# Heads of weight chunks, the order of two mixers, and the row counts of the score products in a two-layer decoder trunk

## The chip, the cores and the metric

The kernel runs on one core of a Trainium2 chip. The metric is the device time of one execution in microseconds (us); the time given for a kernel is the median of its runs. TensorE (PE in the profile) multiplies, ScalarE (ACT) and VectorE (DVE) do element-wise work, GpSimd (POOL) as well, and SyncE (SP) issues the transfers of the weights from the chip's main memory. SBUF is the working memory with 128 partitions, PSUM the memory of eight banks into which TensorE writes.

## The reference

The input is 256 rows of 1024 float32 numbers. Two layers follow each other, each made of a feed-forward block, a mixer and another feed-forward block, all with RMS norm ahead of them and added to the running sum; a final norm ends it.

```python
h = x
for layer in range(DEPTH):
    h = h + 0.5 * swiglu(rms_norm(h, ffn1_norm[layer]), ...)
    hn = rms_norm(h, mix_norm[layer])
    h = h + (ab_mixer(hn, ...) if layer % 2 == 0 else c_mixer(hn, ...))
    h = h + 0.5 * swiglu(rms_norm(h, ffn2_norm[layer]), ...)
return rms_norm(h, final_norm)

def swiglu(x, w_gate, w_up, w_down):
    return (jax.nn.silu(x @ w_gate) * (x @ w_up)) @ w_down
```

`swiglu` goes from 1024 to 2816 and back. The first mixer has two halves: causal attention with 8 heads of 64, in which three windows are combined (they become one mask here), and a gating in which 4 groups of 128 channels are mixed over positions and multiplied with a GELU. The second mixer is causal attention with 16 heads of 64; with 256 rows its blocks are one block. Both end in an output projection.

## The kernel before, in words

**Precision.** A product of two float32 matrices is made of three fast products: each operand is split in a high part (a rounded copy, made by ACT) and a low part (what is left, made by DVE), and `mm3` (lines 197 to 200) adds high x high, high x low and low x high in PSUM. Lines 198, 199 and 200 are these three, so most of TensorE's time stands on them in equal parts.

**Weights.** `Stream` (lines 39 to 112) brings the weights in chunks of 2048 numbers per partition (1 MB). `add` lists the chunks in the order of use, `load_one` issues a transfer on SP's queue, `split_parts` makes the high and low tiles (`whi`, `wlo`; lines 86 and 87). Three raw buffers and four pairs of split ones go round: `take` hands out the next chunk, `free` gives it back and starts later ones. A chunk of a column-wise product has 8 blocks k of 128 input rows and 256 columns, that is two tiles of 128 columns; one tile takes 8 x 3 = 24 matmuls of 256 columns, a chunk 48.

**Heads.** A chunk lies shifted by SHIFT = 16 numbers within lines of 64. Some chunks have `reset=3` (a head): their first three k, all 256 columns of them, are put behind the others, at a place 52 numbers into a line (lines 77 to 80). In a feed-forward block these are the chunks named by `again` (lines 140 to 144): 1 and 3 in the first block, 2 and 3 in the next two, 2, 3 and 7 in the last. Other heads lie in the mixers (lines 165, 166 and 177).

**Feed-forward block** (`ffn`, line 427). Chunk n is taken at step n; gate and up chunks take turns, 22 in all. In the blocks after the first, the sums of squares for the norm are made by small matmuls after chunk 1 (`sums`, line 264), and after chunk 2 two transposes spread them over the columns (`spread`, line 282). In the first block transposes of gain vectors with 16 rows (line 373) come after chunk 2 as well, and in the last one sixteen transposes after chunk 6 (line 444). The down projection has 528 matmuls of 256 columns, in the last block products of 512 columns (`finish`).

**Mixers.** Two kinds of products come by turns. `token_block` (line 689) makes 128 rows of positions by 512 columns: 48 matmuls of 512 columns in two chunks; `tile_of` (line 806) makes 128 columns by 256 positions: 24 matmuls of 256. Between them stand the attention's steps: `put_q` and `put_k` take a tile of two heads from PSUM, `scores(h)` multiplies, applies the mask, the exponential and its scaling, `turn(h)` transposes the probabilities, and `weighted(p)` multiplies a pair of heads with v. A dictionary by slot, written out by hand, says at which slot each is issued (lines 768 to 781 and 829 to 834); a slot is a tile, a part of a token block or a step of the projection. Each engine takes its instructions in the order written (a scheduler moves few of them).

**Scores.** A head has 64 channels. `put_q` puts the high and the low part of q in the two halves of 128 partitions; `put_k` makes a tile with the high part of k in both halves and one with the low part in both (two copies each by POOL, lines 624 and 625). Two 128-row products (lines 637 and 638) for each half of the positions then hold all four combinations.

**Output projection** (`project`, line 308). Four steps of 24 matmuls, then four of 12, then the rest; each uses one block of the mixers' outputs, and `after(i)` runs the events of a slot behind step i. `Next.pair` adds the result to the running sum and makes the input of the next block. The first feed-forward chunk of a block is taken in the order `LATE` (line 306), so that the last two k come late.

Of the kernel before, what the change touches and what calls it, by code (L numbers as in the profile page):

```python
# [10 lines left out]
F32 = mybir.dt.float32  # L11
# [26 lines left out]

class Stream:
# [30 lines left out]
    def split_parts(self):  # L70
# [9 lines left out]
        self.parts[j] = tuple([t[:, at(k) : at(k) + w] for k in range(nk)] for t in (his, los))  # L80
        k0 = 0
        for k1 in cuts:
            a, n = at(k0), int((k1 - k0) * w)
            r = raw[:, int(k0 * w) : int(k0 * w) + n]
            hi, lo = his[:, a : a + n], los[:, a : a + n]
            nc.scalar.activation(hi, r, AF.Copy)  # L86
            nc.vector.tensor_sub(lo, r, hi.bitcast(F32))  # L87
            k0 = k1
            yield
# [26 lines left out]
def trunk(ctx: ExitStack, tc: tile.TileContext, a, out):  # L116
# [473 lines left out]
    def make_attention(mp, mask_cols, nheads, v, mix, engine, rows=False):  # L590
# [6 lines left out]
        def scaled(bk):  # L597
            t = mp.tile([128, S], F32, name="qk", bufs=2)
            nc.vector.tensor_mul(t, bk[:, :S], norm["row"])
            return t  # L600

        def put_q(p, bk):

            qq = mp.tile([128, 2 * S + LINE], F32R, name="q", bufs=pairs)
            t = bk[:, :S] if rows else scaled(bk)
            for j in range(2):
                q = qq[:, SHIFT + j * S : SHIFT + (j + 1) * S]
                r = slice(j * 64, j * 64 + 64)
                o = slice(64 - j * 64, 128 - j * 64)
                nc.scalar.activation(q[r, :], t[r, :], AF.Copy)  # L610
                nc.vector.tensor_sub(q[o, :], t[r, :], q[r, :].bitcast(F32))  # L611
                qs[2 * p + j] = q

        def put_k(p, bk):

            t = scaled(bk)
            for j in range(2):
                kh = mp.tile([128, S], F32R, name=f"kh{j}", bufs=pairs)
                kl = mp.tile([128, S], F32R, name=f"kl{j}", bufs=pairs)
                r = slice(j * 64, j * 64 + 64)  # L620
                o = slice(64 - j * 64, 128 - j * 64)
                nc.scalar.activation(kh[r, :], t[r, :], AF.Copy)
                nc.vector.tensor_sub(kl[r, :], t[r, :], kh[r, :].bitcast(F32))  # L623
                nc.gpsimd.tensor_copy(kh[o, :], kh[r, :].bitcast(F32))
                nc.gpsimd.tensor_copy(kl[o, :], kl[r, :].bitcast(F32))
                ks[2 * p + j] = (kh, kl)

        def scores(h):
            q = qs.pop(h)
            kh, kl = ks.pop(h)  # L630
# [53 lines left out]
    def run_events(ev, s):  # L684
        for f in ev.pop(s, []):
            f()


    def token_block(m, evict, step=lambda: None):

        pb = [bank(), bank()]
        for i in range(2):
# [6 lines left out]
            if i == 0 and m == 0:  # L699
                nxt.sums()  # L700
# [11 lines left out]
    def ab_mixer(phase):  # L712
        with tc.tile_pool(name="mp", bufs=1) as mp:
# [38 lines left out]
            token_block(0, lambda t, p: put_v(v, t, p))  # L752
            nxt.spread()
            token_block(1, keep_g)

# [12 lines left out]
            ev = {}  # L768

            def at(s, f, *args):  # L770
                ev.setdefault(s, []).append(lambda: f(*args))

            at(0, turn_spatial)
            for i, s in enumerate((3, 4, 5, 6)):
                at(s, mixing, i)
            for h, s in enumerate((8, 9, 10, 11, 12, 12, 13, 13)):
                at(s, scores, h)
            for h, s in enumerate((11, 11, 12, 13, 14, 14, 15, 15)):
                at(s, turn, h)
            for p, s in enumerate((12, 14, 15, 16)):  # L780
                at(s, weighted, p)

            slot = 0

            def tiles(put):

                nonlocal slot
                w = st.take()
                for j in range(2):
                    p = bank()  # L790
                    tile_of(p, w, j)
                    put(j, p)
                    run_events(ev, slot)
                    slot += 1
                st.free()
# [5 lines left out]
            for put, c in ((put_u, 0), (put_q, 0), (put_u, 1), (put_k, 0), (put_q, 1), (put_k, 1)):  # L801
# [99 lines left out]
```

## Time and profile before

| what | value |
|---|---|
| median of 3 runs | 978.74 us (978.63 to 981.01) |
| the profiled execution by its own time | 977.56 us |
| its span, from the first to the last instruction | 975.8 us |
| mean granted TensorE clock | 0.997 |
| first mixer, with its projection | 196.3 to 294.1 us |
| second mixer, with its projection | 668.0 to 782.9 us |
| the rest | four feed-forward blocks |

The profile is one execution. In the page's first part stand busy time, its share of the span and the number of instructions of each engine; PEld is the loading of weights (of the operand that is held in the array), which overlaps PE. A matmul lasts 0.28 us in the trace, but the next one begins earlier: what counts is the distance between two starts. A row of the timeline has start, length, engine, line, operation, output and inputs, sizes and, in brackets, idle time ahead of it and what ended it. In a row of the windows stand the stretch, its length, busy time and number by engine (PE, PEld, DVE, ACT, POOL), the granted clock, the share of the DMA engines and GB/s. A row of the waits says who waited for whom: total, times and longest. In a group's row stand line, engine, operation, output and inputs, sizes, count, then busy time, the mean of one in ns, and idle time ahead of it.

### The profile page before, as it was taken

Reading aid. Unit: us, or ns where it says so; the run is one execution under the profiler, and the core shown is the slowest. Engines: PE = TensorE matmul, PEld = TensorE weight load, DVE = VectorE, ACT = ScalarE, POOL = GpSimd, SP = SyncE. Lnnn points to the kernel's source line nnn. Section 1 sums busy time; section 2 is a strip of 40 time slices with the busy share of each in tenths; the row PEclk is TensorE's granted clock in tenths of the full one; section 3 lists DMA queues with packets and bytes.
Section 4 is the critical chain, followed back from the end, with each engine's and each line's share of the span. In section 5 each row is a group of like instructions: output and inputs, shape, how many; then the busy total and the mean of one; then the engine's idle time right before and its main releaser. Section 6 shows DMA issues by size and latency. Waiting matters only on the chain.

```text
span 975.8 us, 18069 instructions
## 1 busy us (share of the span) xinstructions
PE 960.6 (98%) x7679; PEld 935.7 (96%) x7679; DVE 614.5 (63%) x867; ACT 504.4 (52%) x784; POOL 68.4 (7%) x98
## 2 busy tenths in 40 slices
PE   9999999999899999999999999999999999999997
PEld 8999999989899999999999999999999999999886
DVE  6856546568877665655665566466888776566443
ACT  7644444465875544444454444445777665444431
POOL 0000000001400000000000000000466200000000
PEclk9999999999999999999999999999999999999999
DMA  9866555674445655546665664656534466565521
GB/s 294 271 195 192 164 183 173 217 222 164 130 131 182 200 180 180 190 161 202 195 191 178 187 202 152 194 173 224 173 130 130 130 195 194 174 194 174 199 103 44
DMA packets 153537, 174.86 MB, mean 179 GB/s; under 512 B 3008, under 2 KB 142192, under 8 KB 153456
## 3 DMA queue, kind: packets, MB, share of 16 engines
q1 hardware_dynamic: 151888, 171.54, 55.1%
q10 hardware_dynamic: 1568, 2.17, 0.7%
q8 instruction: 60, 0.98, 0.4%
q14 instruction: 21, 0.17, 0.0%
HBM read 172.65 MB, written 1.05 MB: 178 GB/s over the span
## 4 chain that ended last, share of the span: by engine, by line
PE 84%; DVE 6%; ACT 5%; issue 3%; POOL 1%; DMA 1%; POOLq 0%; SPq 0%; ACTq 0%; DVEq 0%
PE bank L198 26%; PE bank L199 26%; PE bank L200 26%; DVE wlo L87 3%; ACT whi L86 2%; PE bank L516 2%; PE bank L513 2%; PE bank L512 2%; ACT pr L644 1%; DMA raw<-in_ffn_w_gate 1%; DVE ptl L204 1%; DVE kl L623 0%; ACT pr L651 0%; DVE q L611 0%; DVE pr L641 0%
## 5 line engine op out<-in xcount | busy, mean ns | idle before, releaser
L86 ACT ACTIVATE whi<-raw 128x1024 fp32r<-128x1024 f32 (+2 forms) x334 | 329.0, 1027 | 394.9 <-issue 304.5
L87 DVE TENSOR_TENSOR wlo<-raw,whi 128x1024 fp32r<-128x1024 f32 (+2 forms) x334 | 387.6, 1192 | 139.7 <-ACT whi L86 138.1
L198 PE MATMUL bank<-xTh,whi 128*128 128x256 f32 x1632 | 458.8, 281 | 0.7 <-ACT whi L86 0.7
L199 PE MATMUL bank<-xTl,whi 128*128 128x256 f32 x1632 | 457.6, 280 | 0.5 <-DVE xTl L236 0.5
L200 PE MATMUL bank<-xTh,wlo 128*128 128x256 f32 x1632 | 457.6, 280 | 0.2 <-DVE wlo L87 0.2
L200 PEld LDWEIGHTS bank<-xTh,wlo 128*128 128x128 f32 x1632 | 311.7, 191 | 0.8 <-DVE wlo L87 0.6
L198 PEld LDWEIGHTS bank<-xTh,whi 128*128 128x128 f32 x1632 | 306.4, 188 | 1.0 <-ACT whi L86 0.9
L199 PEld LDWEIGHTS bank<-xTl,whi 128*128 128x128 f32 x1632 | 306.5, 188 | 0.8 <-DVE xTl L236 0.7
L200 PE MATMUL bank<-hTh,wlo 128*128 128x256 f32 x528 | 148.5, 281 | 0.0
L199 PE MATMUL bank<-hTl,whi 128*128 128x256 f32 x528 | 148.5, 281 | 0.0
L198 PE MATMUL bank<-hTh,whi 128*128 128x256 f32 x528 | 148.5, 281 | 0.0
L200 PEld LDWEIGHTS bank<-hTh,wlo 128*128 128x128 f32 x528 | 101.4, 192 | 0.0
L198 PEld LDWEIGHTS bank<-hTh,whi 128*128 128x128 f32 x528 | 99.1, 188 | 0.0
L199 PEld LDWEIGHTS bank<-hTl,whi 128*128 128x128 f32 x528 | 99.1, 188 | 0.0
L455 DVE TENSOR_TENSOR hm<-gs,bank 128x512 f32<-128x512 f32 x44 | 30.1, 687 | 88.3 <-PE bank L200 88.0
L452 DVE TENSOR_TENSOR gs<-bank,row 128x512 f32<-128x512 f32 x44 | 30.0, 689 | 54.6 <-PE bank L200 54.6
L207 POOL TENSOR_TENSOR rstd<-ms,half_neg 128x2 f32<-128x2 f32 x6 | 5.8, 966 | 634.4 <-DVE ms L266 436.4
L198 PE MATMUL bank<-mixh,whi 128*128 128x256 f32 x128 | 36.7, 287 | 0.0
L199 PE MATMUL bank<-mixl,whi 128*128 128x256 f32 x128 | 36.5, 285 | 0.0
L200 PE MATMUL bank<-mixh,wlo 128*128 128x256 f32 x128 | 36.3, 284 | 0.0
L653 POOL TENSOR_SCALAR pr<-pr,rl 128x128 f32<-128x128 f32 (+1 forms) x32 | 30.2, 958 | 21.0 <-DVE rl L647 15.0
L204 DVE TENSOR_TENSOR hTl<-hm,hTh 128x512 fp32r<-128x512 f32 x44 | 30.2, 685 | 2.1 <-ACT hTh L203 2.1
(135 smaller groups left out, 865.6 us busy)
## 6 DMA issues: line engine op xcount, KB each, us to landing
raw<-in_ffn_w_gate SPq DMA_DIRECT2D x42, 1024.0 KB, 5.4
raw<-in_ffn_w_up SPq DMA_DIRECT2D x42, 1024.0 KB, 5.4
raw<-in_ffn_w_down SPq DMA_DIRECT2D x35, 1024.0 KB, 5.2
raw<-in_c_w_in SPq DMA_DIRECT2D x12, 1024.0 KB, 5.2
raw<-in_ab_w_in SPq DMA_DIRECT2D x10, 1024.0 KB, 5.1
raw<-in_ffn_w_down SPq DMA_DIRECT2D x12, 768.0 KB, 4.4
raw<-in_ab_w_out SPq DMA_DIRECT2D x4, 1024.0 KB, 5.0
raw<-in_c_w_out SPq DMA_DIRECT2D x4, 1024.0 KB, 5.0
```

What stands on the lines that cost most here:

```text
L86: nc.scalar.activation(hi, r, AF.Copy)
L87: nc.vector.tensor_sub(lo, r, hi.bitcast(F32))
L198: nc.tensor.matmul(p, sh, mh, start=start, stop=False)
L199: nc.tensor.matmul(p, sh, ml, start=False, stop=False)
L200: nc.tensor.matmul(p, sl, mh, start=False, stop=stop)
L204: nc.vector.tensor_sub(lo, src, hi.bitcast(F32))
L452: nc.vector.tensor_mul(g, both(pg), twice(norm["row"]))
L455: nc.vector.tensor_mul(hm, g, both(pu))
L512: nc.tensor.matmul(banks[t, h], sh, w[0][kw][:, cs], start=k == 0, stop=False)
L513: nc.tensor.matmul(banks[t, h], sh, w[1][kw][:, cs], start=False, stop=False)
L516: nc.tensor.matmul(banks[t, h], sl, w[0][kw][:, cs], start=False, stop=k == FT - 1)
L653: engine.tensor_scalar(pr[:, cs], pr[:, cs], rl[:, b : b + 1], None, op0=ALU.mult)
```

## The change

It has three parts.

1. **Heads for the first tile alone.** Of the first three k of a headed chunk, the columns of the first tile go to the far place (52 numbers into a line); those of the second tile stand ahead of the tail at the usual 16. `Halves` gives the right one for a slice of columns. The three pieces are split separately. Which chunks have heads is the same in the feed-forward blocks; in the mixers it is another list.
2. **q and k first.** Both mixers begin with the first q chunk and the first k chunk (`first_tiles`), with `sums` between them and `spread` behind them, and hold the four tiles in PSUM until then; `norm["score"]` is now made in both. The token blocks come after, with slots of their own. `Slots` replaces the two dictionaries, and all slots are written anew.
3. **Scores as one 128-row and one 64-row product.** q has its high part in both halves of the partitions (two copies each by POOL), k its high part in one half and its low part in the other; the first product gives high x high and high x low. The second multiplies the low part of q with the high part of k on 64 rows. Low x low is left out. The low part of k is made by POOL.

```diff
+class Halves:
+    def __init__(self, *parts):
+        self.parts = parts
+    def __getitem__(self, key):
+        return self.parts[key[1].start // 128]
...
-        cuts = (*((reset,) if reset else ()), *(cuts or (() if reset else (nk / 2,))), nk)
+        cuts = (*(cuts or (() if reset else (nk / 2,))), nk)
...
+        h = w // 2
+        far = nk * w - reset * h + RESHIFT // LINE * LINE + RESHIFT
         def at(k):
-            return int((k - reset) * w) + shift if k >= reset else int((nk - reset + k) * w) + RESHIFT
+            return int(k * w) - reset * h + shift
+        def part(t, k):
+            if k >= reset:
+                return t[:, at(k) : at(k) + w]
+            return Halves(*(t[:, a : a + h] for a in (far + k * h, shift + k * h)))
...
+        if reset:
+            r = raw[:, : reset * w].rearrange("p (k c) -> p k c", k=reset)
+            split(far, r[:, :, :h])
+            split(shift, r[:, :, h:])
...
     wab = a["ab_w_in"][0]
+    add_cols(wab, 0, 256)
+    add_cols(wab, 512, 256, reset=RESET)
     add_cols(wab, 1024, 512)
     add_cols(wab, 2048, 512)
-    for c in (1536, 0, 1792, 512):
-        add_cols(wab, c, 256, reset=RESET)
-    for c in (256, 768):
-        add_cols(wab, c, 256)
+    for c, n in ((1536, RESET), (1792, 0), (256, RESET), (768, RESET)):
+        add_cols(wab, c, 256, reset=n)
...
-    add_cols(wc, 2048, 512)
     for c in range(4):
-        if c == 2:
-            add_cols(wc, 2560, 512)
-        add_cols(wc, c * 256, 256, reset=0 if c % 2 else RESET)
-        add_cols(wc, 1024 + c * 256, 256)
+        add_cols(wc, c * 256, 256, reset=RESET if c % 2 else 0)
+        add_cols(wc, 1024 + c * 256, 256, reset=0 if c else RESET)
+        if c % 2 == 0:
+            add_cols(wc, 2048 + c * 256, 512)
...
         def put_q(p, bk):
+            t = bk[:, :S] if rows else scaled(bk)
+            q1 = mp.tile([128, S], F32R, name="q1", bufs=2)
+            ql = mp.tile([128, S + LINE], F32R, name="ql", bufs=pairs)[:, SHIFT : SHIFT + S]
             qq = mp.tile([128, 2 * S + LINE], F32R, name="q", bufs=pairs)
-            t = bk[:, :S] if rows else scaled(bk)
+            split(q1, ql, t)
             for j in range(2):
                 q = qq[:, SHIFT + j * S : SHIFT + (j + 1) * S]
...
-                nc.scalar.activation(q[r, :], t[r, :], AF.Copy)
-                nc.vector.tensor_sub(q[o, :], t[r, :], q[r, :].bitcast(F32))
-                qs[2 * p + j] = q
+                r, o = sides(j)
+                for to in (r, o):
+                    nc.gpsimd.tensor_copy(q[to, :], q1[r, :].bitcast(F32))
+                qs[2 * p + j] = (q, ql[r, :])
...
         def put_k(p, bk):
...
-                nc.scalar.activation(kh[r, :], t[r, :], AF.Copy)
-                nc.vector.tensor_sub(kl[r, :], t[r, :], kh[r, :].bitcast(F32))
-                nc.gpsimd.tensor_copy(kh[o, :], kh[r, :].bitcast(F32))
-                nc.gpsimd.tensor_copy(kl[o, :], kl[r, :].bitcast(F32))
-                ks[2 * p + j] = (kh, kl)
+                k = mp.tile([128, S], F32R, name=f"k{j}", bufs=pairs)
+                r, o = sides(j)
+                nc.scalar.activation(k[r, :], t[r, :], AF.Copy)
+                nc.gpsimd.tensor_sub(k[o, :], t[r, :], k[r, :].bitcast(F32))
+                ks[2 * p + j] = (k, k[r, :])
...
-                nc.tensor.matmul(sc[:, b * S : (b + 1) * S], q[:, bs], kh, start=True, stop=False)
-                nc.tensor.matmul(sc[:, b * S : (b + 1) * S], q[:, bs], kl, start=False, stop=True)
+                nc.tensor.matmul(sc[:, b * S : (b + 1) * S], q[:, bs], k, start=True, stop=False)
+                nc.tensor.matmul(sc[:, b * S : (b + 1) * S], ql[:, bs], kh, start=False, stop=True)
...
+    def first_tiles(put_q, put_k, step):
+        ps4 = [bank() for _ in range(4)]
+        w = st.take()
+        for j, ks in LATE:
+            tile_of(ps4[j], w, j, ks)
+        for _ in range(2):
+            step()
+        st.free()
+        nxt.sums()
+        w = st.take()
+        for j in range(2):
+            tile_of(ps4[2 + j], w, j)
+            step()
+        nxt.spread()
...
+        for j in range(2):
+            put_q(j, ps4[j])
+            put_k(j, ps4[2 + j])
+        st.free()
...
+            slots.at((9,), lambda _: turn_spatial())
+            slots.at((14, 15, 16, 17), mixing)
+            slots.at((5, 6, 7, 8, 20, 20, 21, 21), scores)
+            slots.at((8, 9, 10, 11, 22, 22, 23, 23), turn)
+            slots.at((11, 13, 24, 25), weighted)
...
+            first_tiles(put_q, put_k, step)
+            token_block(lambda t, p: put_v(v, t, p), step)
+            token_block(keep_g, step)
+            for put, c in ((put_u, 0), (put_u, 1), (put_q, 1), (put_k, 1)):
+                tiles(put, c, step)
+            project(mix, MIX1, phase, step)
...
+            slots.at((5, 6, 7, 8, 12, 13, 14, 15, 16, 17, 18, 19, 24, 24, 25, 25), scores)
+            slots.at((8, 9, 10, 11, 15, 16, 17, 18, 19, 20, 21, 22, 26, 26, 27, 27), turn)
+            slots.at((11, 13, 18, 20, 22, 24, 28, 29), weighted)
...
             for c in range(4):
+                if c:
+                    tiles(put_q, c, step)
+                    tiles(put_k, c, step)
+                else:
+                    first_tiles(put_q, put_k, step)
+                if c % 2 == 0:
+                    token_block(lambda t, p: put_v(v, t, p, c * 256), step)
+            project(mix, MIX2, phase, step)
```

More of the change, by code (lines that the diff above doesn't have):

```diff
@@ L617, in put_k @@
             for j in range(2):
[L618 to L622, printed above, removed]
[L623 to L626 removed]
+                k = mp.tile([128, S], F32R, name=f"k{j}", bufs=pairs)
[3 more added lines that the diff above has]
+                ks[2 * p + j] = (k, k[r, :])
         def scores(h):
[L629 to L630 removed]
+            q, ql = qs.pop(h)
+            k, kh = ks.pop(h)
             sc = bank()
@@ L698, in token_block @@
             st.free()
-            if i == 0 and m == 0:
-                nxt.sums()
         for t in range(NT):
@@ L766, in mixing @@
                 split(mix[0][:, 4 + g], mix[1][:, 4 + g], tmp)
[L768 to L795, printed above, removed]
+            slots = Slots()
+            slots.at((9,), lambda _: turn_spatial())
[3 more added lines that the diff above has]
+            slots.at((11, 13, 24, 25), weighted)
             def put_u(i, p):
@@ L799, in put_u @@
                 nc.scalar.activation(uT[:, i, :], uT[:, i, :], AF.Gelu_apprx_tanh)
-            for put, c in ((put_u, 0), (put_q, 0), (put_u, 1), (put_k, 0), (put_q, 1), (put_k, 1)):
-                tiles(lambda j, p: put(2 * c + j, p))
-            project(mix, MIX1, phase, lambda i: run_events(ev, 12 + i))
-            assert not ev
-    def tile_of(p, w, j):
-        cs = slice(j * 128, (j + 1) * 128)
-        for k in range(KD):
-            mm3(p[:, :S], w[0][k][:, cs], w[1][k][:, cs], xT["h"][:, k], xT["l"][:, k], k == 0, k == KD - 1)
+            step = slots.step
+            first_tiles(put_q, put_k, step)
[4 more added lines that the diff above has]
+            project(mix, MIX1, phase, step)
+            assert not slots.events
     def c_mixer(phase):
```

84 lines of the change are left out of this document (39 added, 45 removed).

## The prediction

> **What bounds the kernel now.** I read the page first, for the engine that sets the end, and then the windows, for how fast that engine runs in each stretch.
>
> ```profile
> span 975.8 us, 18069 instructions
> ...
> PE 960.6 (98%) x7679; PEld 935.7 (96%) x7679; DVE 614.5 (63%) x867; ACT 504.4 (52%) x784; POOL 68.4 (7%) x98
> ...
> PE 84%; DVE 6%; ACT 5%; issue 3%; POOL 1%; DMA 1%; POOLq 0%; SPq 0%; ACTq 0%; DVEq 0%
> ```
>
> TensorE is busy throughout and carries the chain of work that ended last; nothing else is near its limit. So the time is the number of matmuls times their spacing, plus the gaps. The windows give the spacing.
>
> ```profile
> 30.00:190.00 160.00, 160.00 (x1361) 160.00 (x1360) 97.40 (x107) 74.52 (x92) 0.00 (x0) 1.00 0.61 193
> 317.00:480.00 163.00, 163.00 (x1387) 163.00 (x1386) 95.62 (x104) 73.55 (x90) 0.00 (x0) 1.00 0.59 187
> 504.00:667.00 163.00, 163.00 (x1386) 163.00 (x1385) 95.58 (x104) 72.76 (x89) 0.00 (x0) 1.00 0.59 187
> 804.00:822.00 18.00, 18.00 (x161) 18.00 (x161) 12.94 (x16) 10.11 (x13) 0.00 (x0) 1.00 0.56 176
> 196.30:294.10 97.80, 94.03 (x684) 87.73 (x683) 73.87 (x156) 69.85 (x153) 14.18 (x20) 0.98 0.51 161
> 668.00:782.90 114.90, 112.61 (x839) 105.81 (x839) 93.35 (x204) 81.89 (x180) 48.58 (x65) 1.00 0.46 149
> ```
>
> The columns are the stretch, its length, busy time and count by engine (PE first), the granted clock and DMA. The first four rows lie in feed-forward blocks, where every matmul has 256 columns. A matmul lasts 0.28 us, so some 2.4 of each count began ahead of the stretch. Without these the spacing is 160/1358.6 = 0.1178 us in the first row, the same in the next two, and 18/158.6 = 0.1135 us in the fourth. The clock is 1.00 in all four, and the fourth has the same operations. So there are **two rhythms**, 4.3 ns apart, and each lasts. What starts the change between them is seen one matmul at a time, in chunk 3 of the second feed-forward block. It has a "head": its first three k are put at another place in the 64-element line.
>
> ```profile
> 311.16 0.38 PE L282 MATMUL bank<-ident,wide 128*128 128x128 f32 x2
> 311.30 0.36 PE L198 MATMUL bank<-xTh,whi 128*128 128x256 f32 x1
> ...
> 312.32 0.28 PE L200 MATMUL bank<-xTh,wlo 128*128 128x256 f32 x1
> ...
> 312.55 0.28 PE L199 MATMUL bank<-xTl,whi 128*128 128x256 f32 x1
> ...
> 314.02 0.28 PE L200 MATMUL bank<-xTh,wlo 128*128 128x256 f32 x1
> 314.14 0.28 PE L198 MATMUL bank<-xTh,whi 128*128 128x256 f32 x1
> ...
> 315.19 0.28 PE L198 MATMUL bank<-xTh,whi 128*128 128x256 f32 x1
> ...
> 316.84 0.28 PE L200 MATMUL bank<-xTh,wlo 128*128 128x256 f32 x1
> ```
>
> The first tile's head runs from 311.30 to 312.32. The 13 spacings from 312.55 to 314.02 then take 1.47 us, 0.113 each: fast. At 314.14 the second tile begins, with its own head (the same three k, other columns). The 14 spacings from 315.19 to 316.84 take 1.65 us, 0.118 each: slow, and slow it stays (row 317 to 480). So a head does not set the fast rhythm; it **turns one into the other**. The last block bears this out from the other side:
>
> ```profile
> 801.93 0.28 PE L198 MATMUL bank<-xTh,whi 128*128 128x256 f32 x1
> ...
> 803.58 0.28 PE L200 MATMUL bank<-xTh,wlo 128*128 128x256 f32 x1
> ```
>
> Here the first tile stayed slow after its head (14 spacings, 1.65 us). The second tile's head turned it to fast, and fast it ran to the next transposes (row 804 to 822), across three chunk borders.
>
> **The change, part by part.** *Heads for the first tile alone.* The second tile loses its head and lies, like the tail, at the common shift. What was turned to fast by the first tile then stays fast. Now slow, and behind a turned first tile after the change, are 24 matmuls of chunk 1, the 48 of chunk 2 and, from the second tile of chunk 3, 24 + 18 x 48 + 528 in block one (1488); 24 + 24 + 18 x 48 + 528 in block two (1440); the same and 48 of the entry in block three (1488); in the last block 24 + 15 + 24 + 14 x 48 up to its down projection (735; its 512-column products are no part of this). That is 5151 x 4.3 ns = **-22.1 us**. The bounds are 0, if the fast rhythm is lost at once, and -22.1; I take the full value, since both rhythms cross chunk borders undisturbed in the rows above. A headed chunk is split in three pieces in place of two on ACT and DVE; these are busy 73.55 and 95.62 of 163 us in the feed-forward row, and this is hidden there. The weight DMAs on SP's queue stay 1 MB each and as many; only their order changes.
>
> *Scores.* Each head had two 128-row products per half; now the second has 64 rows. The count is the same, but 128 and 64 rows alternate. The trace has one place where the row count changes, the gains' transposes (16 rows), seen on the weight loads:
>
> ```profile
> 26.01 0.25 PEld L282 LDWEIGHTS bank<-ident,wide 128*128 128x128 f32 x2
> 26.42 0.19 PEld L373 LDWEIGHTS bank<-ident,gr 16*128 16x128 f32 x2 [0.17 <-issue]
> 26.64 0.19 PEld L198 LDWEIGHTS bank<-xTh,whi 128*128 128x128 f32 x1
> ```
>
> ```profile
> 221.70 0.46 PEld L731 LDWEIGHTS bank<-ident,wsp 128*128 128x128 f32 x4
> 222.13 0.19 PEld L198 LDWEIGHTS bank<-xTh,whi 128*128 128x128 f32 x1
> ```
>
> With equal rows the next load starts 0.03 us ahead of the end of the last (222.16 to 222.13). Into 16 rows it waits 0.17 for nothing that the profile names, and out of them 26.61 to 26.64 = 0.03. Against the control that is 0.20 + 0.06 for two switches, 0.13 each. Four switches for each of 24 heads make 96 x 0.13 = **+12.5 us**. The lower end is 0 (64 rows may not behave as 16 do). The upper one is a product whose load nothing hides, as at 311.30: 0.36 in place of 0.113, 96 x 0.25 = 24 us. I take 12.5, from the only row that shows a switch. The Trainium skill, "TensorEngine Tiling (Array Packing)", section Key Properties, states that changing the tiling mode drains TensorE; it gives no price. The 0.17 us agrees with it, and it speaks against this part.
>
> *Mixers: first q and k at once, schedule of slots.* The gaps are the difference of length and PE busy: 97.80 - 94.03 = 3.8 us in the first mixer, 114.90 - 112.61 = 2.3 in the second.
>
> ```profile
> PE bank L661 <- ACT pr L651: 1.6, 1, 1.6
> PE bank L661 <- DVE ptl L204: 1.5, 1, 1.5
> ```
>
> ```profile
> 259.50:263.50 4.00, 4.00 (x24) 4.00 (x23) 3.52 (x11) 3.95 (x11) 2.50 (x4) 0.59 0.17 33
> ```
>
> The 1.6 us is the transpose of a head whose probabilities ACT has not scaled yet; the granted clock then falls to 0.59 and 24 matmuls take 4.0 us in place of 2.7. Four of the eight heads now go into the token blocks, where a slot lasts 12 512-column matmuls. So this wait and the 1.3 us behind it go, and I count half of the second: -3.6. What stays is the tail, where four heads still pass ACT between the first and fourth quarter of the projection:
>
> ```profile
> L644 ACT ACTIVATE pr<-pr,nm 128x128 f32<-128x128 f32 (+1 forms) x48 | 21.4, 446 | 3.7 <-DVE nm L641 3.4
> L651 ACT ACTIVATE pr<-pr,rl 128x128 f32<-128x128 f32 (+1 forms) x16 | 6.2, 443 | 0.3 <-DVE rl L647 0.3
> ```
>
> Their exponentials and scalings alone are 4 x 4 x 0.445 = 7.1 us, beside 72 matmuls (8.2 us) and the chunks' copies on the same queue: late next is the transpose behind them. The second mixer gives half of its 2.3: -1.1. The entry now meets its last two k after 36 matmuls of 0.1135 (4.1 us), before after 24 twice as long (5.4): +0.2, taken twice as the bound. Bounds of the mixers together: -7.4 (all gaps and the clock) to about +4; I take **-4.5**. On POOL each pair of heads had four casts; now it has four for q and two subtractions for k:
>
> ```profile
> L624 POOL CAST kh<-kh 64x256 fp32r<-64x256 f32 x24 | 15.0, 626 | 50.0 <-ACT kh L622 48.9
> L625 POOL CAST kl<-kl 64x256 fp32r<-64x256 f32 x24 | 12.8, 532 | 1.4
> L653 POOL TENSOR_SCALAR pr<-pr,rl 128x256 f32<-128x256 f32 x16 | 18.7, 1169 | 0.0
> ```
>
> That was 2 x (0.626 + 0.532) = 2.3 us a pair and becomes 4 x 0.53 to 0.63 plus two of 0.53 to 1.17 (two-input form not in the trace): 3.2 to 4.8. For the eight pairs of the second mixer POOL goes from 48.58 to between 56 and 69 of 115 us. Behind a subtraction that waits on ACT stand the scalings of older heads, and for those the transposes wait, three slots (about 10 us) on. This covers it; without the cover it is the +4 above. DVE loses two subtractions a pair, ACT one copy, both off the path. Four q and k tiles, sums, spread and a token block hold eight PSUM banks at most.
>
> **Sum.** -22.1 + 12.5 - 4.5 = -14.1 us. The profiled execution took 977.56 us by its own time (span 975.8); the median of the runs is 978.74, 1.2 higher. The forecast is made on the median: **964.6 us**.
>
> **Rivals.** (1) *No switch cost*: 64 rows need no wait. 978.7 - 26.6 = 952. For it: the 16-row operations are float32 transposes, another kind. Against it: the control of equal rows has no such idle time. (2) *Full price*: each score product waits for the one ahead and for its load, 0.20 to 0.25 a switch, 19 to 24 us: 971 to 976. (3) *The rhythm does not hold, and no switch cost*: a border or the down projection, whose fast rhythm the trace never shows, turns it back early: 974. (4) **Slower**: the same loss with the 12.5 us of the scores, 978.7 - 4.5 + 12.5 = 987. Its place is the first chunk after chunk 3, its price the 22.1 us, and it decides once less than 8 us of these are left, so if fast is lost within the first 36% of the matmuls. The Trainium skill, "TensorE: Matmul & The Clock Gate", Part 2, says that loading weights takes no read bandwidth from the running matmul, by which a place in the line could not matter, the first term would be nil and the time that of this rival; 0.1178 against 0.1135 speaks against that rule here. That the heads do not do what they are moved for is (3) and (4).
>
> **How the numbers follow.** Forecast 0.35 (960 to 968), (1) 0.25 (949 to 955), (2) 0.13, (3) 0.10, (4) 0.13, and 0.04 for POOL holding up the mixers. All but (4) and that remainder lie in 947 to 977, 0.83 in all; this is the range. A measurement tells about 0.3%, 2.9 us, from no change. Faster by more: the forecast, (1), most of (2) and (3): 0.80; within: 0.05; slower: 0.15.
>
> **What would show it.** In the feed-forward stretches some 1438 matmuls per 163 us in place of 1387 (first term right), or 1387 (wrong). The second tile of chunk 3 at 0.113. The weight loads of the 64-row products with idle time ahead of them that ends on "issue", or spaced at 0.113 (rival 1). No granted clock under 1.00 in the first mixer. POOL as releaser of TensorE in the second mixer would make the third term wrong; a head that leaves the slow rhythm as it is, as at 801.93, would take some 6 us of the first term in its block.

## The result and the profile after

| | before | after |
|---|---|---|
| median of 4 runs each, same chip | 978.68 us (977.5 to 981.01) | **966.22 us** (965.29 to 967.12) |
| the profiled execution by its own time | 977.56 us | 965.54 us |
| ratio, with its 95% interval | | 0.987 (0.9848 to 0.9891) |

The kernel became faster by 12.5 us; the forecast was 14.1. The sum came out nearly right, but two of its three terms did not: the scores cost some 6.7 us more than forecast, and the mixers gave some 4.9 us more. Where each microsecond lies is seen when the span of the profiled execution is cut where the blocks begin:

| stage, us | before | after | difference | forecast |
|---|---|---|---|---|
| first feed-forward block | 196.27 | 190.03 | -6.24 | -6.4 |
| first mixer | 97.85 | 99.95 | +2.10 | |
| second feed-forward block | 186.78 | 181.03 | -5.75 | -6.2 |
| third feed-forward block | 187.05 | 180.54 | -6.51 | -6.4 |
| second mixer | 114.95 | 122.63 | +7.68 | |
| last block, to the end | 192.94 | 189.63 | -3.31 | -3.2 |
| blocks together | | | **-21.8** | -22.1 |
| mixers together | | | **+9.8** | +8.0 (12.5 - 4.5) |

First the page of the kernel after: the span, the busy line and the chain.

```profile
span 963.8 us, 18092 instructions
...
PE 952.8 (99%) x7679; PEld 916.9 (95%) x7679; DVE 599.3 (62%) x848; ACT 502.2 (52%) x789; POOL 88.2 (9%) x122
...
PE 94%; DVE 2%; issue 1%; ACT 1%; DMA 1%; POOL 0%; SPq 0%; POOLq 0%
```

TensorE has as many matmuls as before (7679), is busy 7.8 us less, and carries 94% of the chain in place of 84%: the chain hardly leaves it any more. The windows of the kernel after, four in feed-forward blocks and then the two mixers, show both halves of the result.

```profile
30.00:185.00 155.00, 155.00 (x1370) 155.00 (x1369) 97.78 (x111) 74.91 (x93) 0.00 (x0) 1.00 0.64 202
317.00:465.00 148.00, 148.00 (x1308) 148.00 (x1307) 90.88 (x100) 68.51 (x84) 0.00 (x0) 1.00 0.60 190
497.00:645.00 148.00, 148.00 (x1309) 148.00 (x1308) 90.31 (x100) 67.99 (x84) 0.00 (x0) 1.00 0.60 189
820.00:897.00 77.00, 77.00 (x682) 77.00 (x681) 46.92 (x49) 35.44 (x42) 0.00 (x0) 1.00 0.60 189
190.03:289.98 99.95, 97.80 (x684) 87.94 (x683) 68.88 (x149) 69.23 (x154) 21.43 (x28) 1.00 0.48 158
651.56:774.19 122.63, 122.42 (x841) 108.41 (x839) 81.95 (x183) 78.93 (x175) 61.15 (x81) 1.00 0.43 140
```

As before, some 2.4 matmuls of each count began ahead of the stretch. 148/(1308 - 2.4) = 0.1134 us, 155/1367.6 and 77/679.6 = 0.1133: all four blocks run in the fast rhythm, to their ends. In the mixers the number of matmuls is the same as before, and TensorE is busy 97.80 us in place of 94.03 in the first and 122.42 in place of 112.61 in the second. The idle time (length less busy time) has shrunk from 3.8 to 2.2 us and from 2.3 to 0.2, and the clock of the first mixer, 0.98 before, is 1.00.

The timeline of TensorE in the kernel after, at the place where the prediction found the change of rhythm (chunk 3 of the second feed-forward block):

```profile
307.56 0.38 PE L308 MATMUL bank<-ident,wide 128*128 128x128 f32 x2
307.70 0.36 PE L224 MATMUL bank<-xTh,whi 128*128 128x256 f32 x1
...
308.72 0.28 PE L226 MATMUL bank<-xTh,wlo 128*128 128x256 f32 x1
...
308.95 0.28 PE L225 MATMUL bank<-xTl,whi 128*128 128x256 f32 x1
...
310.43 0.28 PE L226 MATMUL bank<-xTh,wlo 128*128 128x256 f32 x1
310.54 0.28 PE L224 MATMUL bank<-xTh,whi 128*128 128x256 f32 x1
...
313.15 0.28 PE L226 MATMUL bank<-xTh,wlo 128*128 128x256 f32 x1
```

The first tile's head runs from 307.70 to 308.72; from 308.95 to 310.43 there are 13 spacings, 0.114 each. At 310.54 the second tile begins, now without a head: its 23 spacings to 313.15 take 2.61 us, 0.1135 each. Before, the same tile fell to 0.118 here.

The timeline of TensorE around one head's scores in the first mixer, again of the kernel after, and then its weight loads:

```profile
212.53 0.39 PE L226 MATMUL bank<-whi,xTl 128*128 128x512 f32 x1
212.75 0.28 PE L664 MATMUL bank<-k,q 128*128 128x256 f32 x1
212.96 0.38 PE L665 MATMUL bank<-k,ql 64*128 64x256 f32 x1
213.27 0.39 PE L664 MATMUL bank<-k,q 128*128 128x256 f32 x1
213.59 0.38 PE L665 MATMUL bank<-k,ql 64*128 64x256 f32 x1
213.90 0.51 PE L224 MATMUL bank<-whi,xTh 128*128 128x512 f32 x1
214.24 0.40 PE L225 MATMUL bank<-wlo,xTh 128*128 128x512 f32 x1
```

```profile
212.53 0.19 PEld L664 LDWEIGHTS bank<-k,q 128*128 128x128 f32 x1
212.96 0.18 PEld L665 LDWEIGHTS bank<-k,ql 64*128 64x128 f32 x1 [0.24 <-issue]
213.27 0.19 PEld L664 LDWEIGHTS bank<-k,q 128*128 128x128 f32 x1
```

The first 128-row load begins with the matmul ahead of its own (212.53 against 212.75): it is loaded ahead. From then on every load begins at the same time as its own matmul (212.96, 213.27): here nothing is loaded ahead across a change of the row count. The 64-row load has 0.24 us of idle time in front of it that ends on "issue". From one product to the next it takes 0.21 us the first time and then 0.31 or 0.32, and the four take 213.90 - 212.75 = 1.15 us. The product behind them takes 214.24 - 213.90 = 0.34 us.

### The profile page after: what moved, and what is told of

The parts are those of the page before. It is cut to its first block, busy times and chain, and to the rows that moved or that the text cites. A ratio compares the mean times of both kernels' runs of the same rounds, so it can differ in the third digit from the quotient of the medians.

```text
span 963.8 us, 18092 instructions
## 1 busy us (share of the span) xinstructions
PE 952.8 (99%) x7679; PEld 916.9 (95%) x7679; DVE 599.3 (62%) x848; ACT 502.2 (52%) x789; POOL 88.2 (9%) x122
## 4 chain that ended last, share of the span: by engine, by line
PE 94%; DVE 2%; issue 1%; ACT 1%; DMA 1%; POOL 0%; SPq 0%; POOLq 0%
PE bank L224 28%; PE bank L225 28%; PE bank L226 28%; PE bank L539 2%; PE bank L542 2%; PE bank L538 2%; PE bank L665 2%; DVE wlo L106 1%; PE bank L664 1%; PE bank L688 1%; DMA raw<-in_ffn_w_gate 1%; DVE xTl L262 0%; ACT whi L105 0%; DVE acc L283 0%; POOL q L642 0%
## 5 line engine op out<-in xcount | busy, mean ns | idle before, releaser
L105 ACT ACTIVATE whi<-raw 128x1024 fp32r<-128x1024 f32 (+4 forms) x350 | 331.3, 990 | 382.6 <-issue 290.3
L106 DVE TENSOR_TENSOR wlo<-raw,whi 128x1024 fp32r<-128x1024 f32 (+4 forms) x350 | 390.1, 1147 | 140.7 <-ACT whi L105 139.9
L224 PE MATMUL bank<-xTh,whi 128*128 128x256 f32 x1632 | 453.2, 278 | 0.8 <-ACT whi L105 0.8
L225 PE MATMUL bank<-xTl,whi 128*128 128x256 f32 x1632 | 452.0, 277 | 0.1
L226 PE MATMUL bank<-xTh,wlo 128*128 128x256 f32 x1632 | 451.5, 277 | 0.2 <-DVE wlo L106 0.2
L226 PEld LDWEIGHTS bank<-xTh,wlo 128*128 128x128 f32 x1632 | 306.7, 188 | 0.6 <-DVE wlo L106 0.6
L225 PE MATMUL bank<-hTl,whi 128*128 128x256 f32 x528 | 145.9, 276 | 0.0
L226 PE MATMUL bank<-hTh,wlo 128*128 128x256 f32 x528 | 145.8, 276 | 0.0
L224 PE MATMUL bank<-hTh,whi 128*128 128x256 f32 x528 | 145.8, 276 | 0.0
L642 POOL CAST q<-q 64x256 fp32r<-64x256 f32 x48 | 27.9, 580 | 198.3 <-ACT q L229 196.7
```

The costliest lines, as they stand in the source:

```text
L224: nc.tensor.matmul(p, sh, mh, start=start, stop=False)
L225: nc.tensor.matmul(p, sh, ml, start=False, stop=False)
L226: nc.tensor.matmul(p, sl, mh, start=False, stop=stop)
L642: nc.gpsimd.tensor_copy(q[to, :], q1[r, :].bitcast(F32))
```

## The experiments

Two questions were open. Do the heads alone make the -21.8? And do the mixers' +9.8 come from 96 switches (changes of the row count from one matmul to the next) at more than I had put on them, with a larger gain elsewhere, or from something else? Each experiment undoes one part, or does one alone. Each was timed beside the kernel before, whose median lay between 978.6 and 980.3 us in these rounds, so a difference of two experiments is good to some 1.6 us; what is read finer is read from the stages of one profiled execution each.

**Heads alone.** The kernel before with `Stream` and `Halves` of after (part 1; the `add` lists stay those of before).

```diff
-        cuts = (*((reset,) if reset else ()), *(cuts or (() if reset else (nk / 2,))), nk)
+        cuts = (*(cuts or (() if reset else (nk / 2,))), nk)
...
+            split(far, r[:, :, :h])
+            split(shift, r[:, :, h:])
```

> The kernel before with part 1 alone (heads for the first tile). Theory: the fast rhythm now holds through the feed-forward blocks, -21.8 us there as in the changed kernel, and little changes in the mixers: 955 to 959 us. Rival (the gain needs the new order of chunks or the entry with q and k as well): 965 or more.

Measured: 956.34 us (956.14 to 956.37); ratio 0.9759 (0.9744 to 0.9773). Its blocks are shorter than those of before by 6.41, 6.23, 6.52 and 3.08 us, 22.2 together, and its windows in the second block give the fast rhythm:

```profile
317.00:465.00 148.00, 148.00 (x1308) 148.00 (x1308) 89.87 (x98) 68.52 (x84) 0.00 (x0) 1.00 0.61 192
```

Part 1 by itself makes the kernel faster than the whole change does.

**Old heads.** The counter-test is the kernel after with `Stream` of before, so with heads for both tiles.

```diff
-class Halves:
...
-            split(far, r[:, :, :h])
-            split(shift, r[:, :, h:])
```

> The changed kernel with heads on both tiles as before. Theory: the second tile's head turns the feed-forward blocks back to 0.1178 us a matmul, +20 to +23 us: 986 to 989. Rival (something else in the change made the rhythm last): within 3 us of the changed kernel, 963 to 969.

Measured: 989.3 us (984.49 to 990.29); ratio 1.0086 (1.0057 to 1.0115), 23.1 more than after. The window of its second block:

```profile
317.00:480.00 163.00, 163.00 (x1387) 163.00 (x1386) 97.12 (x107) 74.42 (x93) 0.00 (x0) 1.00 0.58 182
```

163/1384.6 = 0.1177, the slow rhythm of before, with the same count of matmuls. The first term is shown from both sides, and parts 2 and 3 without it make the kernel slower, by 0.9%. One of the four runs, at 984.49, lies some 5 us under the others; it has no trace.

**Two switches a head in place of four.** The kernel after, with the two 128-row products of a head first and then the two 64-row ones; the same products, in another order (`sc[...]` stands for the same part of the bank as in the change).

```diff
-            for b in range(2):
-                bs = slice(b * 128, b * 128 + 128)
-                nc.tensor.matmul(sc[...], q[:, bs], k, start=True, stop=False)
-                nc.tensor.matmul(sc[...], ql[:, bs], kh, start=False, stop=True)
+            for i, (x, y) in enumerate(((q, k), (ql, kh))):
+                for b in range(2):
+                    bs = slice(b * 128, b * 128 + 128)
+                    nc.tensor.matmul(sc[...], x[:, bs], y, start=i == b == 0, stop=i == b == 1)
```

> The changed kernel with the score products in another order: the two 128-row ones of a head, then the two 64-row ones, so two switches a head in place of four. Theory (each switch costs 0.20 us): 48 x 0.20 = 9.6 us go, 955 to 959. Rival (a 64-row product is slow in itself, not the switch): unchanged, 964 to 968.

Measured: 956.27 us (955.75 to 956.55); ratio 0.9757 (0.974 to 0.9774), 9.95 less than after. Its mixers take 96.80 and 116.21 us, 3.15 and 6.42 less for 16 and 32 switches less: 0.20 for each in both. Its timeline (two products in a row, x2):

```profile
212.51 0.40 PE L665 MATMUL bank<-k,q 128*128 128x256 f32 x2
212.84 0.50 PE L665 MATMUL bank<-k,ql 64*128 64x256 f32 x2
213.27 0.50 PE L224 MATMUL bank<-whi,xTh 128*128 128x512 f32 x1
```

A head's four products take 213.27 - 212.51 = 0.76 us in place of 1.15, so 0.39 less for two switches. This fixes the price with only the order of the four products changed: **0.20 us**. At that price 96 switches cost 19.2 us, not 12.5.

**No switch: the low part beside zeros.** The kernel after, with the low part of q in tiles of 128 rows whose other half is zero, so that the second product too has 128 rows and takes the whole k. What is computed stays that of after. It costs one subtraction more on DVE for each pair of heads (`PAD` is true), and the zeros' room is taken from `tmp`.

```diff
+            for i in range(pairs if rows else 2):
+                low = mp.tile([128, 2 * S + LINE], F32R, name=f"low{i}")
+                nc.gpsimd.memset(low.bitcast(F32), 0.0)
...
+                    nc.vector.tensor_sub(low[r, :], t[r, :], q1[r, :].bitcast(F32))
...
-                ks[2 * p + j] = (k, k[r, :])
+                ks[2 * p + j] = (k, k if PAD else k[r, :])
...
-                tmp = mp.tile([128, NT, 128], F32, name="tmp", bufs=2)
+                tmp = mp.tile([128, NT, 128], F32, name="tmp", bufs=1)
```

> The changed kernel with a second score product of 128 rows: the low part of q stands beside 64 rows of zeros, and the whole k tile is the moving operand, so no row count changes. ACT and POOL do what they do in the changed kernel; DVE has one more subtraction a pair, and one buffer is single. Theory: the 19 us of the switches go and the lighter copies keep the waits away, 947 to 951. Rival (what the old scores got back as waits comes from TensorE being ahead, whoever copies): 952 to 956. If the switches only fill waits: 960 or more.

Measured: 954.0 us as a median, but the runs lie at two levels, 950.61 and 950.77, 957.22 and 958.02; ratio 0.9743 (0.9703 to 0.9783). The timeline and the windows of its mixers, from the execution at 950.77:

```profile
211.88 0.28 PE L680 MATMUL bank<-k,q 128*128 128x256 f32 x1
212.00 0.28 PE L681 MATMUL bank<-k,low 128*128 128x256 f32 x1
...
212.35 0.40 PE L224 MATMUL bank<-whi,xTh 128*128 128x512 f32 x1
212.59 0.40 PE L225 MATMUL bank<-wlo,xTh 128*128 128x512 f32 x1
```

```profile
189.86:287.20 97.34, 92.67 (x684) 85.90 (x683) 70.56 (x153) 68.33 (x154) 22.05 (x30) 1.00 0.50 162
649.00:759.44 110.44, 110.04 (x840) 104.51 (x839) 85.56 (x191) 78.24 (x175) 65.59 (x85) 1.00 0.49 155
```

A head's four products take 212.35 - 211.88 = 0.47 us in place of 1.15, and the product behind them 0.24 in place of 0.34: the last switch is paid there. Together that is 0.78 us for four switches, 0.195 each, which agrees with the price above. TensorE is busy 5.1 and 12.4 us less than in after, 17.5 together, 0.18 a switch. But in the first mixer only 2.6 us of the 5.1 arrive, since its idle time rises from 2.2 to 4.7 us: what the slow products had covered comes out as waits. In the second mixer all but 0.2 us arrive: its idle time is 0.4 us, with the copies of after and quick products. So the rival named above, that the waits come back whoever copies, holds in the first mixer and not in the second.

**The two levels.** The same kernel was profiled again, twice, to see where the 7 us lie.

> padded_all once more, for its second level: four runs took 950.77, 958.02, 950.61 and 957.22. Theory (one feed-forward block that misses the fast rhythm costs 6.2 to 6.5 us): 950.5 to 951 with all blocks at 0.1133 us a matmul, or 957 to 958 with one block at 0.1178. Rival (a wait or the clock in a mixer): all blocks fast at 957.

> padded_all once more, for its second level. Theory: 950.5 to 951 with all blocks fast, or 957 to 958 with one block at 0.1178 us a matmul. Rival: all blocks fast at 957.

Measured: 950.79 and 957.63 us. The stages of the two agree within 0.3 us, but for the second block: 180.79 against 187.15. Its window in the first execution, and in the second one:

```profile
310.00:465.00 155.00, 155.00 (x1370) 155.00 (x1369) 93.92 (x103) 72.10 (x90) 0.00 (x0) 1.00 0.61 192
```

```profile
310.00:465.00 155.00, 155.00 (x1319) 155.00 (x1318) 91.70 (x101) 69.53 (x86) 0.00 (x0) 1.00 0.58 184
```

155/1316.6 = 0.1177 against 155/1367.6 = 0.1133: in one execution, with the same program, a whole block kept the slow rhythm although its first tile has a head. So a head does not turn the rhythm every time. A run of the kernel before at 971.37 us, in another round, lies 7.9 us under the median there, somewhat more than one block; it has no trace.

**The same place.** The kernel after with the head's pieces in the same order, but at 16 numbers into a line like all others.

```diff
-RESET, RESHIFT = 3, 52
+RESET, RESHIFT = 3, 16
```

> The changed kernel with the first tile's head put 16 numbers into a line, where all else lies, in place of 52; split in the same three pieces. Theory (the place turns the rhythm): after the transposes the feed-forward blocks mostly go on slow, 975 to 989, each block all slow or all fast. Rival (the separate split or the order of the pieces does it): 965 to 968.

Measured: 975.87 us (973.21 to 977.38, 8 runs); ratio 0.9966 (0.9954 to 0.9979), 9.7 more than after. The windows of one execution:

```profile
30.00:190.00 160.00, 160.00 (x1361) 160.00 (x1360) 97.47 (x108) 74.55 (x93) 0.00 (x0) 1.00 0.62 194
317.00:470.00 153.00, 153.00 (x1353) 153.00 (x1352) 95.28 (x105) 73.22 (x92) 0.00 (x0) 1.00 0.60 188
497.00:650.00 153.00, 153.00 (x1353) 153.00 (x1352) 95.09 (x105) 72.34 (x91) 0.00 (x0) 1.00 0.61 190
802.00:822.00 20.00, 20.00 (x179) 20.00 (x178) 14.68 (x18) 11.79 (x17) 0.00 (x0) 1.00 0.58 175
826.00:884.00 58.00, 58.00 (x495) 58.00 (x494) 33.30 (x35) 26.18 (x32) 0.00 (x0) 1.00 0.58 182
```

160/1358.6 = 0.1178, 153/1350.6 = 0.1133 twice, 58/492.6 = 0.1177: the first block is slow, the two between are fast, without any operand at another place in its line. The last block is fast before its sixteen transposes (20/176.6 = 0.1132) and slow behind them. The place is worth 9.7 us here, but it isn't the only thing that sets the rhythm. The timeline of the second block shows when it is set; two transposes begin at 315.81, the first tile's head at 315.95 and the matmuls behind the head at 317.07:

```profile
316.39 0.28 PE L224 MATMUL bank<-xTh,whi 128*128 128x256 f32 x1
...
317.52 0.28 PE L225 MATMUL bank<-xTl,whi 128*128 128x256 f32 x1
```

These ten spacings take 1.13 us, 0.113 each, and the first six of them lie ahead of the first matmul behind the head. So here the rhythm is fast from the fourth matmul behind the transposes, not from the end of the head.

**Old scores.** The kernel after with `put_q`, `put_k` and the products of before: parts 1 and 2 without part 3.

```diff
-                for to in (r, o):
-                    nc.gpsimd.tensor_copy(q[to, :], q1[r, :].bitcast(F32))
+                nc.scalar.activation(q[r, :], t[r, :], AF.Copy)
+                nc.vector.tensor_sub(q[o, :], t[r, :], q[r, :].bitcast(F32))
...
-                nc.tensor.matmul(sc[...], q[:, bs], k, start=True, stop=False)
-                nc.tensor.matmul(sc[...], ql[:, bs], kh, start=False, stop=True)
+                nc.tensor.matmul(sc[...], q[:, bs], kh, start=True, stop=False)
+                nc.tensor.matmul(sc[...], q[:, bs], kl, start=False, stop=True)
```

> The changed kernel with the scores of before: two 128-row products, and put_q and put_k as before. Theory: no change of row count, so 24 heads x 0.80 us = 19 us go, less some waits that come back because TensorE is ahead of the other engines: 947 to 953. Rival (ACT, DVE and POOL set the pace of the mixers, and the slow score products only fill waits): 960 to 966.

Measured: 954.2 us (953.65 to 955.24); ratio 0.9738 (0.9723 to 0.9754), 12.0 less than after. That lies between the two expectations: 19.2 us of switches are gone, and 12 arrive. The windows of its mixers and its waits show the rest:

```profile
190.33:287.15 96.82, 93.69 (x684) 87.72 (x683) 73.87 (x161) 70.69 (x157) 12.87 (x20) 0.98 0.49 163
648.93:762.49 113.56, 110.75 (x840) 104.54 (x839) 93.71 (x207) 81.64 (x183) 48.24 (x65) 1.00 0.47 151
```

```profile
PE bank L664 <- POOL kl L651: 2.8, 4, 0.9
PE bank L687 <- POOL pr L679: 1.7, 3, 0.8
```

TensorE is idle for 3.1 and 2.8 us (2.2 and 0.2 in after), now for POOL, whose copies and scalings come too late when the products are quick, and the clock of the first mixer is 0.98 again. This accounts for 3.5 us of the 7.2, and the clock for about 1.3 (in this trace too, from 262 to 266 us, 24 matmuls take 4.0 us in place of 2.7, at a clock of 0.57); some 2.4 us I can't assign.

**Scores alone.** The kernel before with the scores of after: part 3 without 1 and 2.

```diff
-                nc.tensor.matmul(sc[...], q[:, bs], kh, start=True, stop=False)
-                nc.tensor.matmul(sc[...], q[:, bs], kl, start=False, stop=True)
+                nc.tensor.matmul(sc[...], q[:, bs], k, start=True, stop=False)
+                nc.tensor.matmul(sc[...], ql[:, bs], kh, start=False, stop=True)
```

> The kernel before with part 3 alone (128-row and 64-row products, its put_q and put_k). Theory: +19 us for the switches, less waits of the mixers that slower score products and fewer copies cover (4 to 9 us): 988 to 994. Rival (only the new order lets the waits go): 997 to 999. Rival (no such price): 978 or less.

Measured: 986.26 us (985.5 to 987.25); ratio 1.0071 (1.0051 to 1.0091), 7.6 more than before and a little under what was expected. Its mixers:

```profile
196.62:294.05 97.43, 97.36 (x685) 88.03 (x683) 68.63 (x144) 67.96 (x149) 21.29 (x28) 1.00 0.50 162
668.11:791.22 123.11, 123.03 (x841) 108.87 (x840) 82.40 (x180) 78.84 (x173) 63.69 (x81) 1.00 0.43 139
```

In the old order, with the old slots, the slow products take away all the waits: idle 0.07 and 0.08 us, clock 1.00. The first mixer does not become longer at all (97.43 against 97.85). So what the prediction expected of part 2 is done by part 3 alone, and part 2 finds nothing left. Set side by side, both mixers together take, in us (both kernels of the first row have the new heads, both of the second the old ones, so each row is to be read across):

| | slots of before | slots of after |
|---|---|---|
| products of before | 213.8 (heads alone) | 210.4 (old scores) |
| products of after | 220.5 (scores alone) | 224.1 (old heads) |

With the products of before part 2 gains 3.4; with those of after it loses 3.6.

**One slot later.** The kernel without switches has its longest waits at the spatial mixing of the first mixer (`vn`, made by DVE) and at scores whose k POOL has not made. Mixing, the first four scores and what follows them go one slot later.

```diff
-            slots.at((14, 15, 16, 17), mixing)
-            slots.at((5, 6, 7, 8, 20, 20, 21, 21), scores)
-            slots.at((8, 9, 10, 11, 22, 22, 23, 23), turn)
-            slots.at((11, 13, 24, 25), weighted)
+            slots.at((15, 16, 17, 18), mixing)
+            slots.at((6, 7, 8, 9, 20, 20, 21, 21), scores)
+            slots.at((9, 10, 11, 12, 22, 22, 23, 23), turn)
+            slots.at((12, 14, 24, 25), weighted)
```

> The kernel with zeros beside the low part of q (padded_all), with the first four scores, their transposes and the mixing of the first mixer one slot later. Its trace had TensorE wait 1.2 us for the k tiles ahead of the first scores and 2.1 us for vn ahead of the first mixing. Theory (these waits are lateness of ACT, DVE and POOL by less than a slot): 3 us less than padded_all, 947 to 949 in the better of its two levels, and the level at 957 moves to 954 if it shows. Rival (the waits move to the next slot): 950 to 951.

> padded_later once more, for its second level (948.3 to 949 and 955.0 were measured). Theory: 948 to 949 with all feed-forward blocks at 0.1133 us a matmul, or 954 to 956 with one block at 0.1178. Rival (a wait or the clock in a mixer): all blocks fast at 955.

Measured: **948.67 us** (948.27, 948.44, 948.90 and once 955.00); ratio 0.9718 (0.9657 to 0.9778), and 948.43 in a single run on another chip. It is the fastest of all. The longest waits of the kernel without switches, and then its own longest one:

```profile
PE bank L845 <- DVE vn L839: 2.1, 1, 2.1
PE bank L680 <- POOL k L668: 1.5, 2, 1.0
```

```profile
PE bank L680 <- POOL k L668: 2.3, 2, 2.0
```

The wait for `vn` is gone from the list; the one for POOL's k is not, and it grew from 1.5 to 2.3 us. The first mixer takes 95.8 us in place of 97.3, so of the 3 us that were expected some 2 came. The run at 955.00 is 6.5 over the others, as much as one block in the slow rhythm; that it was this is only argued, since that run has no trace.

## Why the prediction came out right, and where it did not

The forecast of 964.6 us lay 1.6 below the median, and the likeliest case was the one that occurred in the sum. Term by term:

- **Heads, -22.1: right.** The blocks gave -21.8, and part 1 alone -22.2 in the blocks. Each block agrees with its own count of matmuls within 0.5 us, and the rate fits too: 1308 matmuls in 148 us are 1440 in 163, and the prediction named 1438. What made this possible is that both rhythms stood in the trace before the change, with the borders that they cross. Rivals (3) and (4), by which the rhythm is lost early, fell.
- **"A head turns one rhythm into the other": not enough.** In the profile of after each block is fast, but the second execution of the kernel without switches has a head that left its block slow, and with the heads at the common place two blocks are fast nevertheless, and were so before the head had ended. Nor do the two rhythms decide what rival (4) set against them, whether weight loads take anything from the running matmul: both occur with every operand at the same place in its line. The risk that the prediction named ("some 6 us of the first term in its block") is real and has this size, 6.4 us. What decides on the rhythm when a block begins stays open.
- **Scores, +12.5: mis-sized.** The failed step is 0.13 us a switch, taken from the small transposes of 16 rows. A score product costs 0.20 a switch: 19.2 us. That is rival (2)'s price, 0.20 to 0.25. Its ground was the better one, a product that waits for the one ahead of it and for its own load, which the loads of after show: they start with their matmul. The 0.20 also stood in the prediction's working, for the switch into 16 rows; averaging it with 0.06 for the switch out of them hid it. The 0.25, though, was read wrongly: it sets the length of the matmul at 311.30, 0.36, against a spacing, 0.113. The next row of the timeline of before gives its spacing, 0.20 us against 0.12, so 0.08 more:

```profile
311.50 0.28 PE L199 MATMUL bank<-xTl,whi 128*128 128x256 f32 x1
```

The time that rival (2) gave, 971 to 976 us, did not come, because of the next term. Rival (1), no cost, fell.
- **Mixers, -4.5: mis-sized, by adding what does not add.** After the switches' 19.2 us, +9.8 leaves -9.4 for everything else. Part 2 with the old products gives -3.4 in the mixers, near the -4.7 forecast for them. Part 1, for which no change was forecast there, adds 1.0 (213.8 against 212.8). The other -7.0 come with part 3: in the order of after it costs 12.2 in the mixers in place of 19.2; in the order of before 7.7. Slower products on TensorE give ACT, DVE and POOL more time, so the waits that part 2 was to remove fill up by themselves. For the first mixer that is shown, since quick products bring the waits back whichever copies are made (idle 3.1 us with the old scores, 4.7 with zeros, 2.2 in after). In the second it isn't: with quick products TensorE is idle for 2.8 us with the old copies and for 0.4 with those of part 3, so there the copies count. Of the -7.0, waits and clock are 4.8 in the trace of the old scores; the rest stays open. The prediction took the gaps of before as a gain for part 2 and the switches as a cost on top, both in full.
- **Smaller steps.** POOL is busy for 61.15 of 122.63 us in the second mixer, forecast 56 to 69, and TensorE does not wait for it there. The subtraction on POOL takes 0.985 us, forecast 0.53 to 1.17:

```profile
L642 POOL CAST q<-q 64x256 fp32r<-64x256 f32 x48 | 27.9, 580 | 198.3 <-ACT q L229 196.7
L652 POOL TENSOR_TENSOR k<-qk,k 64x256 fp32r<-64x256 f32 x24 | 23.6, 985 | 10.5 <-ACT k L651 9.3
```

The waits for `pr` and `ptl` are gone, also in the tail, where the prediction had kept one as "late next". In their place stand two that it did not name, both in the first mixer:

```profile
PE bank L829 <- DVE vn L823: 1.0, 1, 1.0
PE bank L664 <- POOL k L652: 0.9, 1, 0.9
```

The two errors, +6.7 for the switches and -4.9 for the rest, have one cause in part, since a dearer switch covers more waits; that is in part why the sum held better than its terms. That they met within 1.6 us is luck: nothing in the prediction ties the one to the other.

## What to carry to other kernels

Where the engine that sets the end also waits for others, a cost put on it is first paid out of its waits, and a gain is first lost to them: work out both together, never as a sum of two full amounts. Do not carry the price of a change of form (here the row count) over from a short instruction of another shape (0.13 us became 0.20), and look whether the load starts ahead of its matmul or with it. Compare a length with a length and a spacing with a spacing. When a change has several parts, run the parts alone: here the first part alone was 10 us faster than the whole, and the whole with zeros beside the low part, and some slots one later, another 8 faster than that.

## What the runs showed of the hardware that was not expected

- A product of 256 columns with another row count than those around it starts 0.31 us after the one ahead of it in place of 0.12 (the first of a head 0.21), and each switch costs 0.20 us. Multiplying 64 rows of zeros as well is cheaper (0.47 us for a head's four products in place of 1.15). The Trainium skill, "TensorEngine Tiling (Array Packing)", section Key Properties, states that changing the tiling mode drains TensorE. The loads of after agree with it: at a change between 128 and 64 rows they start with their matmul, not ahead of it (212.96, 213.27).
- The rhythm of a whole feed-forward block, 0.1133 or 0.1177 us, can differ between executions of the same program (block two: 180.79 and 187.15 us). In these blocks it lasts for more than a thousand matmuls; what decides it is open.
- With the heads at the common place, the rhythm is fast in two blocks, slow in one, and in the last it is fast up to the transposes and slow behind them. With the heads of after at 52, one of 36 traced blocks was slow. The place in the line thus makes the fast rhythm more likely; it isn't what makes it possible.
